# A hybrid decoder block on one core: earlier weight loads in the second half of the sparse branch, and a power on GpSimd as seed of the norms

## The chip, the cores and the metric

The kernel runs on one NeuronCore of one Trainium2 chip. What counts is the device time of one execution in microseconds (us). The engines are named as in the profile: PE (TensorE matmul, PEld its weight loads), DVE (VectorE), ACT (ScalarE), POOL (GpSimd) and SP (SyncE, which issues most of the DMAs). Each engine works through its own row of instructions in order; semaphores hold an instruction until what it reads is there.

## The reference, cut to what matters

One decoder block over 1024 tokens and 16 meta tokens of 1024 features, in float32:

```
def rms_norm(x, g):
    y = x * rsqrt(mean(x * x, axis=-1) + EPS)
    return y * g

hn = rms_norm(h, attn_norm_g)
proj = hn @ w_in                      # window q k v, latents of the sparse branch, indexer, gates
q = rms_norm(bq, q_norm_g) @ w_uq
c_kv = rms_norm(bkv, kv_norm_g)
ik = layer_norm(ik, idx_k_ln_g, idx_k_ln_b)
o_a = sliding_window_sink_attention(...)
o_b = indexed_sparse_mla(...)         # top 256 keys of each query, found by the indexer's scores
mixed = gate_a * (o_a @ w_branch_a) + gate_b * (o_b @ w_branch_b)
h = h + mixed @ w_out
hn = rms_norm(h, ffn_norm_g)
h = h + (silu(hn @ w_ffn_gate) * (hn @ w_ffn_up)) @ w_ffn_down
y = rms_norm(h, final_norm_g)
```

Each norm needs a reciprocal square root per token: for the two halves of the input (tiles `rx0`, `rx1`, 128 partitions x 5 columns), for the index keys (`rk`, 128 x 9), for the latents of the sparse branch (`rlat`, 128 x 18), and for each of eight blocks of 128 tokens before the feed-forward part and again at the end (`rh`, 128 x 1).

## The kernel before, in words

All large products are done as three matmuls of a high and a low part: ACT casts a tile to its high part, POOL or DVE subtracts to get the low part (`w_hi`, `w_lo` for weights in `weights`, L168 to L190; `fhl`, `th`, `tl`, `oh`, `ol` for other operands), and PE adds the three products in PSUM (`mm3`, L202).

The program is written as a sequence of phases: the norm of the input (`norm_x`, L398: sums of squares at L415, the mean at L417, `rsqrt` at L418, scaling at L424, PE transposes at L429), the indexer, the gates, the top-k search (`select_topk`, where `count` at L838 is done on DVE in rounds for the longest rows, and ACT, L880, and POOL, L824 and L888, search the others; L825 takes low halves), the latents (`latents`, L595, with `rsqrt` for `rlat` at L589 and the scaling L593), window attention, the sparse attention with the products `branch_a` and the first half of `branch_b`, then `phase_mix` (L1157): the second half of `branch_b`, a Winograd product with `w_out`, the norm before the feed-forward part (`squares` L1252, `row_scale` L1258, the scaling `xs` on ACT L1279, transposes to `s` on PE L1288, the copies `hb` on DVE L1291), the feed-forward part, and the last norm (`final`, L1525: `row_scale`, then `y` on ACT, L1533, with POOL, L1534, or on DVE, L1536).

The order on each engine isn't the order of the text: the whole program is placed by a scheduler that simulates a timeline (L1569), and the tiles' ring buffers (`bufs`) set which instruction must wait for which. So an edit in one place can move instructions in others.

A reciprocal square root is done on DVE alone. `rsqrt` takes a seed by two integer operations on the bits (L219, L220) and three Newton steps of three instructions (L222 to L224). `row_scale` makes `v` (L1264), the same seed (L1266, L1267), and three steps of two instructions (L1269, L1270); what its constants leave in scale is taken back in the gains (-1/256).

In the second half of `branch_b` the eight column blocks of `w_branch_b` are taken in the order of `HALF1` = 4, 5, 6, 7, 0, 1, 2, 3. The blocks 4 to 7 are still in the ring `w` of `WB` = 4 places from the first half. The blocks 0 to 3 are loaded again, each in the loop at its own turn, into that ring. Each unit loads a gate tile `ga` and a tile `gt` of the other branch, multiplies, and adds (`ga` L1140, `gt` L1141 in the profile's lines).

Of the kernel before, what the change touches and what calls it, by code (L numbers as in the profile page):

```python
# [7 lines left out]
F32 = mybir.dt.float32  # L8
F32R = mybir.dt.float32r
BF = mybir.dt.bfloat16  # L10
I32 = mybir.dt.int32
# [3 lines left out]
ALU = mybir.AluOpType  # L15
# [4 lines left out]
P = 128  # L20
D = 1024
KC = D // P
T = 1024
NB = T // P
# [26 lines left out]
WB = 4  # L51
# [52 lines left out]
class Program:  # L104
# [105 lines left out]
                    mm = self.matmul(ps, a, b, start=start and i + k == 0, stop=stop and i == n - 1 and k == 2, **kw)  # L210
        return mm.ins

    def rsqrt(self, pool, v, n, tag, e=0):

        nc = self.nc
        y = pool.tile([P, n], F32, name=f"{tag}_y", tag=f"{tag}_y", bufs=1)
        a = pool.tile([P, n], F32, name=f"{tag}_a", tag=f"{tag}_a", bufs=1)
        yi = y.bitcast(I32)
        nc.vector.tensor_scalar(yi, v.bitcast(I32), 1, None, op0=ALU.logical_shift_right)  # L219
        nc.vector.tensor_scalar(yi, yi, -1.0, float(0x5F3759DF + (e << 23)), op0=ALU.mult, op1=ALU.add)  # L220
        for _ in range(3):
            nc.vector.tensor_mul(a, y, y)  # L222
            nc.vector.scalar_tensor_tensor(a, a, -0.5 / 4 ** e, v, op0=ALU.mult, op1=ALU.mult)
            nc.vector.scalar_tensor_tensor(y, a, 1.5, y, op0=ALU.add, op1=ALU.mult)  # L224
        return y

    def run(self):
# [6 lines left out]
    def setup(self, tmp):  # L234
        nc, I, const = self.nc, self.I, self.const
        self.ident = const.tile([P, P], F32, name="ident")
        make_identity(nc, self.ident)
        rows = sum(n for _, n in VEC_ROWS)
        self.vec = const.tile([P, rows], F32, name="vec")
# [6 lines left out]
        at = 0  # L246
# [11 lines left out]
        nc.tensor.transpose(pt[:, :rows], raw, self.ident[:rows, :rows])  # L258
        nc.vector.tensor_copy(self.vec, pt[:, :rows])
        g = self.col["ffn_norm_g"]  # L260
        nc.vector.tensor_scalar(self.vec[:, g:g + 8], self.vec[:, g:g + 8], -1.0 / 256, None, op0=ALU.mult)
        g = self.col["b_gates"]
        nc.vector.tensor_scalar(self.vec[:, g:g + 16], self.vec[:, g:g + 16], 0.5, None, op0=ALU.mult)
        g = self.col["q_norm_g"]
# [859 lines left out]
    def branch_b(self, half, gp, marks=None):  # L1124

        nc, I, pool = self.nc, self.I, self.wg
        o = self.load_o(pool, self.ob_dram[half], 2, lo_pool=False, ring=gp if half else self.xhp, bufs=4 if half else 8)
        banks = ((self.gp, "gps"), (self.tp, "tp"), (self.sp, "s"), (self.tp, "tp"), (self.sp, "s"))
        for at, m in enumerate(HALF1 if half else range(KC)):
            if half == 0 or m < KC - WB:  # L1130
                self.wb[m] = self.weights(pool, I["w_branch_b"][0][:, P * m:P * m + P].rearrange("(k p) n -> p k n", p=P), raw_pool=pool, unit=512, bufs=WB)
            w = self.wb[m]
            y, g = [gp.tile([P, 512], F32, name=nm, tag=nm, bufs=GB if half else 2) for nm in ("gt", "ga")]
            nc.sync.dma_start(g, self.gate_dram[half][8 + m])
            self.mixed_in = nc.sync.dma_start(y, self.ya_dram[half][m]).ins
            bank, tag = banks[m % len(banks) if half else 0]
            ps = bank.tile([P, 512], F32, name=tag, tag=tag)
            self.mm3(ps, [(*w[k], *o[k]) for k in range(4)], marks)
            if half:
                nc.vector.tensor_mul(g, g, ps)  # L1140
                nc.vector.tensor_add(self.X[f"2{m // 4 + 1}"][:, m % 4], y, g)  # L1141
                self.load_out_weights(at)
            else:
                nm = ("oh", "ol")[m % 2]
                self.mixed.append(self.xhp.tile([P, 512], F32, name=nm, tag=nm, bufs=8))
                nc.vector.tensor_mul(g, g, ps)
                nc.gpsimd.tensor_add(self.mixed[m], y, g)

    def load_out_weights(self, at):

# [107 lines left out]
    def row_scale(self, b):  # L1258


        nc = self.nc
        t = self.hp.tile([P, 3], F32, name="rh", tag="rh", bufs=4)
        v, y, z = [t[:, k:k + 1] for k in range(3)]
        nc.vector.tensor_scalar(v, self.ss[:, b, :1], self.ss[:, b, 1:], D * EPS, op0=ALU.add, op1=ALU.add)  # L1264
        yi = y.bitcast(I32)
        nc.vector.tensor_scalar(yi, v.bitcast(I32), 1, None, op0=ALU.logical_shift_right)  # L1266
        nc.vector.tensor_scalar(yi, yi, -1.0, float(0x5F3759DF), op0=ALU.mult, op1=ALU.add)  # L1267
        for s in (1, 2, 16):
            nc.vector.scalar_tensor_tensor(z, y, y, v, op0=ALU.mult, op1=ALU.mult)  # L1269
            self.scaled_dve = nc.vector.scalar_tensor_tensor(y, z, -3.0 * s * s, y, op0=ALU.add, op1=ALU.mult).ins  # L1270
        return y


# [169 lines left out]
    def ffn_down(self):  # L1443
# [3 lines left out]
        nc, I, kc = self.nc, self.I, NF // 2  # L1447
# [9 lines left out]
        sums, gain = {}, None  # L1457
        for name in ("m1", "m5", "m6", "m3", "m7", "m2", "m4"):
# [47 lines left out]
            if name == "m7":  # L1506
                gain = self.fwp.tile([P, D], F32, name="gain", tag="fs", bufs=2)
                nc.sync.dma_start(gain, I["final_norm_g"].unsqueeze(0).to_broadcast([P, D]))
                nc.gpsimd.tensor_scalar(gain, gain, -1.0 / 256, 1.0, op0=ALU.mult, op1=ALU.mult)
            for k, i in [(k, i) for i in range(4) for k in range(kc)] if last else [(k, i) for k in range(kc) for i in range(4)]:  # L1510
                c = slice(P * i, P * i + P)
                xh, xl, yh, yl = ops[k]
# [60 lines left out]
```

## Time and profile before

| | us |
|---|---|
| runs, median of 3 | 1484.69 |
| runs, lowest and highest | 1483.06, 1485.52 |
| profiled execution | 1482.89 |
| its span in the trace | 1480.7 |
| PE busy | 1380.9 (93% of the span) |
| DVE busy | 1002.8 (68%) |
| ACT busy | 817.0 (55%) |
| POOL busy | 609.9 (41%) |

The span runs from the first to the last instruction that the trace has; the profiled execution's own time is 2.2 us longer. All times below count from the start of the span. A busy PE is the sign of a stretch that PE bounds; where PE is idle, the row of its next instruction names in brackets how long it was idle and what ended the wait.

### The profile page before, as it was taken

How to read it: one execution, taken by the hardware profiler on the slowest of the kernel's cores; microseconds unless marked ns; L12 is line 12 of the kernel's file. 1: busy time of each engine (PE TensorE's matmuls, PEld its weight loads, DVE VectorE, ACT ScalarE, POOL GpSimd, SP SyncE). 2: the span in 40 equal slices, each digit the busy share in tenths (PEclk: the TensorE clock that was granted, in tenths of full speed). 3: DMA queues.
4: the chain of work that ended last, by engine and by line, in shares of the span. 5: the costliest groups of instructions: out<-in, count | busy, mean ns of one | idle time of the engine just before them, and what ended most of it. 6: DMA issues, size and time to landing. Idle time of an engine off the chain costs nothing.

```text
span 1480.7 us, 21298 instructions
## 1 busy us (share of the span) xinstructions
PE 1380.9 (93%) x6847; PEld 1149.3 (78%) x6847; DVE 1002.8 (68%) x2136; ACT 817.0 (55%) x1743; POOL 609.9 (41%) x873
## 2 busy tenths in 40 slices
PE   4999997698998899999899699999999999999997
PEld 3988985586776788888677578888888888888886
DVE  6258979556786796785797984445544547696585
ACT  5347977883896686785246633333333334444473
POOL 4135574446675556664200025554554554000004
PEclk9999999799999899999999899999999999999999
DMA  6421221256336555327912033332322338823332
GB/s 204 144 65 46 57 85 64 69 185 198 100 108 170 147 165 162 118 94 251 307 50 97 18 114 114 115 114 97 109 87 100 107 107 309 309 100 107 120 101 114
DMA packets 148038, 189.79 MB, mean 128 GB/s; under 512 B 11331, under 2 KB 95126, under 8 KB 147670
## 3 DMA queue, kind: packets, MB, share of 16 engines
q1 hardware_dynamic: 147568, 188.28, 39.3%
q8 instruction: 54, 0.88, 0.2%
q14 instruction: 58, 0.48, 0.1%
q0 software_dynamic: 160, 0.01, 0.0%
q10 hardware_dynamic: 198, 0.14, 0.0%
HBM read 133.49 MB, written 58.03 MB: 129 GB/s over the span
## 4 chain that ended last, share of the span: by engine, by line
PE 69%; DVE 14%; DMA 5%; issue 4%; ACT 3%; POOL 3%; SPq 1%; POOLq 0%; DVEq 0%; ACTq 0%
PE ps L193 28%; PE s L193 25%; PE gps L193 9%; DVE mask L838 3%; PE pv L1073 2%; DMA kraw<-bk_dram 1%; PE s L1031 1%; PE tp L1062 1%; PE tp L198 1%; POOL y L1534 1%; DVE ptl L133 1%; DVE pb L1035 1%; PE pv L193 1%; DMA ga<-gate_dram 1%; DVE hb L1291 1%
## 5 line engine op out<-in xcount | busy, mean ns | idle before, releaser
L1384 POOL TENSOR_TENSOR fhl<-fr,fhl 128x512 fp32r<-128x512 f32 x60 | 96.8, 1633 | 224.0 <-ACT fhl L1383 224.0
L1384 POOL TENSOR_TENSOR fhl<-fs,fhl 128x512 fp32r<-128x512 f32 x80 | 106.4, 1353 | 106.6 <-ACT fhl L1383 106.6
L193 PE MATMUL s<-ht,fhl 128*128 128x512 f32 x384 | 121.7, 393 | 0.7 <-ACT fhl L1383 0.4
L188 POOL TENSOR_TENSOR w_lo<-w_raw,w_hi 128x512 fp32r<-128x512 f32 x60 | 80.5, 1343 | 83.5 <-ACT w_hi L187 74.2
L193 PE MATMUL ps<-ht,fhl 128*128 128x512 f32 x320 | 101.1, 392 | 0.0
L193 PE MATMUL gps<-oh,w_hi 128*128 128x512 f32 x232 | 93.8, 404 | 4.5 <-ACT gt L938 4.3
L193 PE MATMUL gps<-ol,w_hi 128*128 128x512 f32 x232 | 92.0, 397 | 0.0
L193 PE MATMUL gps<-oh,w_lo 128*128 128x512 f32 x232 | 91.6, 395 | 0.0
L193 PE MATMUL s<-yhl,fhl 128*128 128x512 f32 x396 | 90.6, 389 | 0.0
L193 PE MATMUL ps<-yhl,fhl 128*128 128x512 f32 x396 | 90.3, 389 | 0.0
L1454 ACT CAST yhl<-wd 128x512 fp32r<-128x512 f32 x66 | 41.1, 622 | 88.1 <-PE ps L193 48.5
L193 PE MATMUL s<-h,fhl 128*128 128x512 f32 x272 | 87.6, 393 | 1.1 <-DVE hb L1291 1.1
L193 PE MATMUL ps<-h,fhl 128*128 128x512 f32 x256 | 82.9, 395 | 5.1 <-ACT h L1341 5.1
L133 DVE TENSOR_TENSOR ptl<-tp,pth 128x512 fp32r<-128x512 f32 (+2 forms) x112 | 70.6, 645 | 24.2 <-ACT pth L127 23.8
L193 PEld LDWEIGHTS s<-yhl,fhl 128*128 128x128 f32 x396 | 74.3, 188 | 15.5
L193 PEld LDWEIGHTS ps<-yhl,fhl 128*128 128x128 f32 x396 | 74.3, 188 | 15.5
L193 PEld LDWEIGHTS s<-ht,fhl 128*128 128x128 f32 x384 | 72.0, 188 | 18.4 <-ACT fhl L1383 1.3
L880 ACT ACTIVATE mask<-high,smallg 128x1040 bf16<-128x1040 int16 (+3 forms) x66 | 70.7, 1071 | 24.0 <-DVE high L825 13.3
L1383 ACT CAST fhl<-fr 128x512 fp32r<-128x512 f32 x66 | 39.8, 619 | 76.3 <-issue 36.1
L1455 DVE TENSOR_TENSOR yhl<-wd,yhl 128x512 fp32r<-128x512 f32 x66 | 45.5, 689 | 49.0 <-ACT yhl L1454 49.0
L193 PE MATMUL s<-lt,fhl 128*128 128x512 f32 x192 | 75.1, 392 | 0.0
L1383 ACT CAST fhl<-fs 128x512 fp32r<-128x512 f32 x88 | 54.6, 625 | 33.1 <-PE s L193 17.4
(496 smaller groups left out, 4203.0 us busy)
## 6 DMA issues: line engine op xcount, KB each, us to landing
fr<-in_w_ffn_gate SPq DMA_DIRECT2D x22, 512.0 KB, 4.0
fr<-in_w_ffn_up SPq DMA_DIRECT2D x22, 512.0 KB, 4.6
wd<-in_w_ffn_down SPq DMA_DIRECT2D x44, 256.0 KB, 5.0
da<-acts SPq DMA_DIRECT2D x44, 256.0 KB, 3.5
w_raw<-in_w_in SPq DMA_DIRECT2D x40, 256.0 KB, 3.1
act<-a SPq DMA_DIRECT2D x33, 256.0 KB, 2.1
da<-act SPq DMA_DIRECT2D x33, 256.0 KB, 3.9
acts<-s SPq DMA_DIRECT2D x33, 256.0 KB, 2.0
```

What stands on the lines that cost most here:

```text
L133: nc.vector.tensor_sub(lo, ps, hi.bitcast(F32))
L188: (nc.vector if lo_dve else nc.gpsimd).tensor_sub(t[1], t[2], t[0].bitcast(F32))
L193: mm = self.nc.tensor.matmul(*args, **kw)
L198: mm = self.nc.tensor.transpose(*args)
L838: nc.vector.tensor_scalar(self.mask[j], src[j], at[:, i:i + 1], None, op0=op, op1=ALU.add, accum_out=out[:, i:i + 1])
L880: nc.scalar.activation(self.mask[j], src[j], AF.Sign, bias=at[:, i:i + 1], scale=scale, accum_out=out[:, i:i + 1])
L1031: nc.tensor.matmul(ps[:, :n], q[k][:, h, qc:qc + P], kb[:, h, at:at + n], start=k == 0, stop=k == 1)
L1073: mm = nc.tensor.matmul(acc[:, e, :], v, t[k][:, 256 * i:256 * i + 256], start=r + i + k == 0, stop=False)
L1383: nc.scalar.copy(hi, a[name])
L1384: (nc.gpsimd if q else nc.vector).tensor_sub(lo, a[name], hi.bitcast(F32))
L1454: nc.scalar.copy(hi, src)
L1455: nc.vector.tensor_sub(lo, src, hi.bitcast(F32))
```

## The change

`rsqrt` takes its seed from one GpSimd instruction, a power with exponent -0.5 out of a constant tile `power`, and does one Newton step. `row_scale` does the same with one step of two instructions, and the gains carry -16. That is 20 power instructions in all. In the second half of `branch_b` the blocks 0 and 1 get places of their own (`wb_hi`, `wb_lo`, in the pool of that phase, with the low part on DVE) and are loaded ahead of the loop; the blocks 2 and 3 are loaded into the ring behind the matmuls of the first two units.

```diff
-    def rsqrt(self, pool, v, n, tag, e=0):
+    def rsqrt(self, pool, v, n, tag):
...
-        yi = y.bitcast(I32)
-        nc.vector.tensor_scalar(yi, v.bitcast(I32), 1, None, op0=ALU.logical_shift_right)
-        nc.vector.tensor_scalar(yi, yi, -1.0, float(0x5F3759DF + (e << 23)), op0=ALU.mult, op1=ALU.add)
-        for _ in range(3):
-            nc.vector.tensor_mul(a, y, y)
-            nc.vector.scalar_tensor_tensor(a, a, -0.5 / 4 ** e, v, op0=ALU.mult, op1=ALU.mult)
-            nc.vector.scalar_tensor_tensor(y, a, 1.5, y, op0=ALU.add, op1=ALU.mult)
+        nc.gpsimd.tensor_tensor(y, v, self.power[:, :n], op=ALU.pow)
+        nc.vector.tensor_mul(a, y, y)
+        nc.vector.scalar_tensor_tensor(a, a, -0.5, v, op0=ALU.mult, op1=ALU.mult)
+        nc.vector.scalar_tensor_tensor(y, a, 1.5, y, op0=ALU.add, op1=ALU.mult)
         return y
...
+        self.power = const.tile([P, 2 * NB + 2], F32, name="power")
+        nc.gpsimd.memset(self.power, -0.5)
...
-        nc.vector.tensor_scalar(self.vec[:, g:g + 8], self.vec[:, g:g + 8], -1.0 / 256, None, op0=ALU.mult)
+        nc.vector.tensor_scalar(self.vec[:, g:g + 8], self.vec[:, g:g + 8], -16.0, None, op0=ALU.mult)
...
+        if half:
+
+            for m in range(2):
+                self.wb[m] = self.branch_weights(gp, m, "wb", 2)
         for at, m in enumerate(HALF1 if half else range(KC)):
-            if half == 0 or m < KC - WB:
-                self.wb[m] = self.weights(pool, I["w_branch_b"][0][:, P * m:P * m + P].rearrange("(k p) n -> p k n", p=P), raw_pool=pool, unit=512, bufs=WB)
+            if half == 0:
+                self.wb[m] = self.branch_weights(pool, m)
...
             if half:
+                if at < 2:
+                    self.wb[2 + at] = self.branch_weights(pool, 2 + at)
                 nc.vector.tensor_mul(g, g, ps)
...
+    def branch_weights(self, pool, m, tag="w", bufs=WB):
+        src = self.I["w_branch_b"][0][:, P * m:P * m + P].rearrange("(k p) n -> p k n", p=P)
+        names = tag if tag == "w" else ("wb_hi", "wb_lo", "w_raw")
+        return self.weights(pool, src, tag=names, raw_pool=self.wg, unit=512, bufs=bufs, lo_dve=tag != "w")
...
         nc.vector.tensor_scalar(v, self.ss[:, b, :1], self.ss[:, b, 1:], D * EPS, op0=ALU.add, op1=ALU.add)
-        yi = y.bitcast(I32)
-        nc.vector.tensor_scalar(yi, v.bitcast(I32), 1, None, op0=ALU.logical_shift_right)
-        nc.vector.tensor_scalar(yi, yi, -1.0, float(0x5F3759DF), op0=ALU.mult, op1=ALU.add)
-        for s in (1, 2, 16):
-            nc.vector.scalar_tensor_tensor(z, y, y, v, op0=ALU.mult, op1=ALU.mult)
-            self.scaled_dve = nc.vector.scalar_tensor_tensor(y, z, -3.0 * s * s, y, op0=ALU.add, op1=ALU.mult).ins
+        nc.gpsimd.tensor_tensor(y, v, self.power[:, :1], op=ALU.pow)
+        nc.vector.scalar_tensor_tensor(z, y, y, v, op0=ALU.mult, op1=ALU.mult)
+        self.scaled_dve = nc.vector.scalar_tensor_tensor(y, z, -3.0, y, op0=ALU.add, op1=ALU.mult).ins
         return y
...
-                nc.gpsimd.tensor_scalar(gain, gain, -1.0 / 256, 1.0, op0=ALU.mult, op1=ALU.mult)
+                nc.gpsimd.tensor_scalar(gain, gain, -16.0, 1.0, op0=ALU.mult, op1=ALU.mult)
```

The scheduler moves more than the diff says. Three places matter below. In the changed kernel a line's number is one lower from the setup up to `branch_b`, and three to ten higher behind it.

On DVE, where the norm of the latents meets the search: `small`, `smallg` and `smalld` are the search's bounds, `high` and `sc` its scores, the 128x784 and 128x528 pieces belong to the rows that ACT and POOL search. Before, ahead of the first round of counts over `smalld`:

```order
261 L846 TENSOR_SCALAR smalld<-smalld 128x3
262 L825 SCALAR_TENSOR_TENSOR high<-high,smallg_1219,mask_149 128x784
263 L825 SCALAR_TENSOR_TENSOR sc_203<-sc_203,smallg_1219,mask_147 128x528
264 L848 TENSOR_SCALAR smalld<-smalld 128x3
265 L825 SCALAR_TENSOR_TENSOR high<-high,small,mask_150 128x912
266 L825 SCALAR_TENSOR_TENSOR high<-high,small,mask_148 128x656
267 L838 TENSOR_SCALAR mask_150,smalld<-high,smalld 128x912
```

and now:

```order
230 L845 TENSOR_SCALAR smalld<-smalld 128x3
231 L847 TENSOR_SCALAR smalld<-smalld 128x3
232 L824 SCALAR_TENSOR_TENSOR high<-high,small,mask_150 128x912
233 L824 SCALAR_TENSOR_TENSOR high<-high,small,mask_148 128x656
234 L837 TENSOR_SCALAR mask_150,smalld<-high,smalld 128x912
235 L824 SCALAR_TENSOR_TENSOR high<-high,small,mask_145 128x272
236 L837 TENSOR_SCALAR mask_148,smalld<-high,smalld 128x656
237 L824 SCALAR_TENSOR_TENSOR high<-high,smallg_1200,mask_149 128x784
238 L837 TENSOR_SCALAR mask_145,smalld<-high,smalld 128x272
239 L824 SCALAR_TENSOR_TENSOR sc_203<-sc_203,smallg_1200,mask_147 128x528
```

The 784 and 528 pieces have moved from ahead of the first round into it. At the search's end the scaled latents (`ck`, `qn`, L135) have moved too: from behind the three L804 and one L811 that follow the search to right behind its last round of counts.

On SP, the DMA issues of the second half of `branch_b`: `ga` and `gt` are its gate and merge tiles, `w_raw` the blocks of `w_branch_b` before they are split. Before:

```order
299 L1135 DMA gt<-ya_dram_99 128x512
300 L1134 DMA ga<-gate_dram_124 128x512
301 L1135 DMA gt<-ya_dram_100 128x512
302 L1134 DMA ga<-gate_dram_140 128x512
303 L1135 DMA gt<-ya_dram_108 128x512
...
307 L185 DMA w_raw<-in_w_branch_b 128x4x128 x2
308 L1134 DMA ga<-gate_dram_134 128x512
```

and now:

```order
297 L185 DMA w_raw<-in_w_branch_b 128x4x128
298 L1138 DMA gt<-ya_dram_107 128x512
299 L185 DMA w_raw<-in_w_branch_b 128x4x128
...
305 L1138 DMA gt<-ya_dram_99 128x512
306 L185 DMA w_raw<-in_w_branch_b 128x4x128
307 L1137 DMA ga<-gate_dram_124 128x512
308 L1138 DMA gt<-ya_dram_100 128x512
309 L1137 DMA ga<-gate_dram_140 128x512
```

The last load of weights stood behind the tiles 124, 140 and 133, and stands now ahead of 124; the four loads are spread out, where the last four came in two pairs.

On DVE, between the Winograd product and the feed-forward part (`rh` is the norm's scale, `hb` the transposed copy of the scaled blocks, `l`, `fs` and `fhl` operands of the feed-forward part). Before, the second four blocks:

```order
1330 L1269 SCALAR_TENSOR_TENSOR rh<-rh 128x1
1331 L1270 SCALAR_TENSOR_TENSOR rh<-rh 128x1
1332 L1267 TENSOR_SCALAR rh<-rh 128x1
1333 L1269 SCALAR_TENSOR_TENSOR rh<-rh 128x1
1334 L1270 SCALAR_TENSOR_TENSOR rh<-rh 128x1
1335 L1269 SCALAR_TENSOR_TENSOR rh<-rh 128x1 x2
...
1348 L1270 SCALAR_TENSOR_TENSOR rh<-rh 128x1 x2
1349 L1291 TENSOR_TENSOR hb_8851<-s,vec 128x4x128
```

and now:

```order
1266 L1277 SCALAR_TENSOR_TENSOR rh<-rh 128x1
1267 L1276 SCALAR_TENSOR_TENSOR rh<-rh 128x1
1268 L1349 TENSOR_TENSOR l_9701<-hb_8823,h_9656 128x512
...
1275 L1277 SCALAR_TENSOR_TENSOR rh<-rh 128x1
1276 L1276 SCALAR_TENSOR_TENSOR rh<-rh 128x1
1277 L1381 TENSOR_TENSOR fs<-fs,fr 128x512
1278 L1277 SCALAR_TENSOR_TENSOR rh<-rh 128x1
1279 L1298 TENSOR_TENSOR hb_8825<-s,vec 128x4x128
```

The run of small instructions ahead of `hb` is gone; two per block are left, spread among the large ones. On PE the 16 transposes of the first two blocks have moved from behind the product's last matmuls to ahead of its last group.

## Rows read from the trace of the kernel before

**Rows 1.** Windows: length; PE, PEld, DVE, ACT, POOL busy us; PE clock; DMA share; GB/s.

```profile
197.00:245.00 48.00, 48.00 (x209) 39.05 (x209) 44.91 (x127) 30.20 (x69) 33.01 (x76) 1.00 0.27 88
245.00:270.00 25.00, 4.76 (x20) 2.99 (x18) 24.10 (x68) 19.80 (x45) 11.25 (x40) 0.65 0.15 52
270.00:300.00 30.00, 28.41 (x121) 22.79 (x122) 10.79 (x18) 26.23 (x59) 13.73 (x46) 0.89 0.20 65
...
700.00:730.00 30.00, 24.75 (x103) 18.35 (x101) 20.01 (x30) 7.96 (x13) 8.90 (x7) 1.00 0.85 281
...
806.00:858.00 52.00, 37.38 (x179) 29.80 (x177) 49.30 (x113) 33.89 (x59) 0.00 (x0) 0.87 0.12 46
858.00:1441.00 583.00, 582.60 (x2544) 477.00 (x2543) 346.76 (x466) 230.98 (x419) 204.54 (x141) 1.00 0.39 133
```

**Rows 2.** Timeline of DVE, 8 to 40 us: start, duration, instruction, idle before.

```profile
12.77 0.17 DVE L417 TENSOR_SCALAR ss<-ss 128x5 f32<-128x5 f32 x1
...
16.92 2.73 DVE L424 TENSOR_SCALAR x<-x,rx_y 128x1024 f32<-128x1024 f32 x4
...
20.89 1.05 DVE L417 TENSOR_SCALAR ss<-ss 128x5 f32<-128x5 f32 x1
...
32.72 2.08 DVE L424 TENSOR_SCALAR x<-x,rx_y 128x1024 f32<-128x1024 f32 x3 [0.26 <-DVE rx_y L224]
```

**Rows 3.** Timeline of PE, 8 to 42 us.

```profile
17.73 0.48 PE L429 MATMUL tp<-ident,x 128*128 128x128 f32 x1 [7.88 <-DVE x L424]
25.55 0.66 PE L429 MATMUL tp<-ident,x 128*128 128x128 f32 x4 [2.01 <-DVE xt L135]
```

**Rows 4.** Groups of POOL: busy us, mean ns of one, idle before.

```profile
L890 POOL TENSOR_TENSOR smallg<-smallg 128x2 f32<-128x2 f32 x64 | 13.6, 213 | 5.0
...
L1534 POOL TENSOR_TENSOR y<-y,gain 128x1024 f32<-128x1024 f32 x5 | 11.9, 2397 | 61.2 <-ACT y L1533 61.2
```

**Rows 5.** Timeline of POOL, 0 to 42 us.

```profile
3.12 0.30 POOL masks.py:199 TENSOR_SCALAR_AFFINE_SELECT ident<-ident 128x128 f32<-128x128 f32 x1
```

**Rows 6.** Timeline of DVE, 185 to 275 us.

```profile
194.37 1.32 DVE L219 TENSOR_SCALAR rlat_y<-ssq 128x18 int32<-128x18 int32 x1
...
197.93 5.73 DVE L593 TENSOR_SCALAR lraw<-lraw,rlat_y 16x128 f32<-16x128 f32 x17
...
206.07 1.02 DVE L825 SCALAR_TENSOR_TENSOR high<-high,smallg,mask 128x784 uint16<-128x784 int16 x1
207.01 0.75 DVE L825 SCALAR_TENSOR_TENSOR sc<-sc,smallg,mask 128x528 uint16<-128x528 int16 x1
...
266.94 0.16 DVE L861 SCALAR_TENSOR_TENSOR small<-smalld,small 128x3 int32<-128x3 int32 x1
...
269.74 0.23 DVE L135 SCALAR_TENSOR_TENSOR ck<-tp,vec,ck 128x16 fp32r<-128x16 f32 x1
```

**Rows 7.** Waits, 245 to 300 us: total us, times, longest.

```profile
PE s L193 <- ACT qn L129: 13.4, 1, 13.4
...
PE tp L198 <- DVE ck L135: 6.9, 1, 6.9
```

**Rows 8.** Timeline of PE, 708 to 732 us.

```profile
717.40 0.50 PE L193 MATMUL s<-oh,w_hi 128*128 128x512 f32 x1 [2.09 <-ACT w_hi L187]
...
728.14 0.97 PE L193 MATMUL ps<-th,fhl 128*128 128x512 f32 x3 [1.55 <-DVE ga L1140]
```

**Rows 9.** Timeline of DVE, 785 to 845 us.

```profile
806.81 2.48 DVE L1291 TENSOR_TENSOR hb<-s,vec 128x512 f32<-128x512 f32 x4 [2.47 <-PE s L1288]
...
822.72 0.34 DVE L1269 SCALAR_TENSOR_TENSOR rh<-rh 128x1 f32<-128x1 f32 x2
...
826.57 0.69 DVE L1291 TENSOR_TENSOR hb<-s,vec 128x512 f32<-128x512 f32 x1 [1.86 <-PE s L1288]
```

**Rows 10.** Timeline of DVE, 1455 to 1482 us.

```profile
1473.37 0.21 DVE L1264 TENSOR_SCALAR rh<-ss 128x1 f32<-128x1 f32 x1 [0.85 <-ACT sq L1256]
...
1475.39 0.75 DVE L1536 SCALAR_TENSOR_TENSOR y<-h,rh,gain 128x512 f32<-128x512 f32 x1
```

## The prediction

> **What bounds the kernel now.** I read the windows first: they show in which stretches PE is full, and there only less PE work helps. From 858 to 1441 us PE is busy for 582.60 of 583.00 us, and from 197 to 245 for 48.00 of 48.00 [rows 1]. The change takes no matmul away, so such a stretch only passes on what was gained ahead of it. The gaps are where something can be won: the start (PE idle for 7.88 us ahead of its first transposes, 2.01 later) [rows 3], 245 to 270 (PE busy 4.76 of 25.00, granted clock 0.65), 700 to 730 (24.75 of 30.00, DMA share 0.85) and 806 to 858 (37.38 of 52.00, with DVE busy 49.30) [rows 1]. The waits and timelines then name what ends each gap. Of 245 to 270 that is one wait of 13.4 us for `qn` and one of 6.9 for `ck`, both by way of DVE [rows 7]; the reader sees `ck` written only at 269.74 [rows 6].
>
> **The price that no row shows** is D, one power on GpSimd, the hops to POOL and back included. The nearest rows are a multiply of 128x2, 0.213 us, and of 128x1024, 2.397 us [rows 4]: a fixed 0.21 and some (2397 - 213)/1022 = 2.1 ns for a column. With k times the work of a multiply for each column, D is about 0.2 + 0.0021 k n us for n columns. At k = 1 that is 0.2 for every use, at k = 100 1.3 for `rx` (5 columns), 4.0 for `rlat` (18) and 0.4 for `rh` (1). I take D = 0.5 all through, nearest to the small row; the ends are 0.2 and the k = 100 values. Nothing below zero is possible, since POOL must start an instruction.
>
> **Start.** The mean is there at 12.77 + 0.17 = 12.94, the scaling of `x` starts at 16.92 [rows 2]: 3.98 us for eleven DVE instructions, with a sum of squares between them. After: D and three instructions. At 3.98 for twelve pieces none takes more than about 0.3 on average, so 1.1 to 1.4, a gain of 2.6 to 2.9 at D = 0.5, and PE's 7.88 shrinks by as much. On POOL only one low part of the indexer's weights stands ahead, done by then. In the second half the mean starts at 20.89 and scaling at 32.72 [rows 2]: nearly 12 us, since the small instructions share DVE with the copies of the first half. Three instead of eleven let go several us earlier, but PE has the first half's work to do then and idles for 2.01 only. I take 3 for the start; 0 to 5 are the ends. The third norm, of the index keys, lies beside PE's full stretch and counts as nothing; if that cover went, it would cost D less eight small instructions, a gain at the D taken.
>
> **Latents and search.** From 194.37 to 197.93 the seed and the steps of `rlat` hold DVE, 3.56 us, the first instruction 1.32 long, so the other ten 0.22 each [rows 6]. After: D and 0.7, a gain of 2.4, or 1.3 if an instruction goes on being slowed as that first one is; I take 1.1, since POOL has other small work ahead of the power. Against it: the two low halves of 1.02 and 0.75 us [rows 6] stood where DVE waited for POOL, and stand now inside the first counting round; 1.8 us on the search's chain, as what is queued behind them is every later round. For it: `ck` and `qn` no longer wait behind the four or so large instructions after the search, between 266.94 and 269.74 [rows 6], so 2.8 us. Net 2 for PE in this stretch. With the start's 3 that would be 5 us at 270. From 270 to 300 PE has 28.41 of 30.00 us of work [rows 1], so it passes on; the mask work behind the search ends only by what the search itself gained (3 + 1.1 - 1.8). I take 4 for all up to window attention, bounds 0 and 8. ACT's half of the search starts its next rows late with those halves: what is late next if its rows become the last.
>
> **Sparse attention.** The scheduler reorders it without a reason in the diff. PE is nearly full there. Zero, plus or minus 3.
>
> **Second half of the branch.** PE waits 2.09 us for `w_hi`, late because its DMA landed late, and later 1.55 for a bank that `ga` on DVE frees [rows 8]. The last weight load now goes out ahead of the tiles 124, 140 and 133 on SP. The bytes are the same, though, and DMA is at 0.85 [rows 1], so the tiles come later by what the weights come earlier: `ga` is late next. Two low parts move from POOL to DVE, 0.69 each as another 128x512 there [rows 9]; DVE is idle for 10 of these 30 us [rows 1], which covers them. If that cover went they would cost 1.4. I take 2; bounds 0 and 4.5, the gap's 5.25 less a rest.
>
> **Norm before the feed-forward part.** DVE is the bound of 806 to 858 (49.30 of 52.00) [rows 1], idle for 2.47 ahead of the first `hb` and 1.86 ahead of the fifth [rows 9]. Six of nine instructions go for each of four blocks, 24 in all; two take 0.34 [rows 9], so up to 24 x 0.17 = 4.1, less where they overlap. The 1.86, a wait for `xs` behind the last `rh`, goes if the powers finish beside the large instructions, which at D = 0.5 they do: POOL has nothing in this stretch (0.00) [rows 1]. The first transposes and copies move ahead of the product's end, into the 2.47. That makes up to 8.4. I take 4, half, since PE's own 37 us must still fit the rest; bounds 0.5 and 7.
>
> **End.** From the end of `v` (1473.37 + 0.21) to `y` at 1475.39 [rows 10] eight instructions take 1.81 us, 0.23 each, all on the path. After: D and two of them. Gain 0.9; bounds -0.5 (D = 1.9) and 1.2. In the blocks before, powers queue on POOL behind four long multiplies, off the path.
>
> **Sum:** 4 + 0 + 2 + 4 + 0.9 = 10.9 us off 1482.89 makes 1472.0 for a profiled execution. That one stands 1.8 below the median of its runs, 1484.69; so I forecast **1474** for the median.
>
> **A rule against the change.** No row of POOL shows a first use that costs extra: the first AFFINE_SELECT took 0.30 [rows 5]. The Trainium skill, page GPSIMD Engine Reference, section 2.1 Instruction dispatch, says that the first call to a freshly loaded kernel pays some 6 us to load its code, with no instruction in the profile for it. By that rule, as an estimate from that page alone, the sum would be 4.9 instead of 10.9; the row of the first AFFINE_SELECT doesn't show such a cost, though it need not be a freshly loaded kernel.
>
> **Rivals.** (1) *The reordering gives it back:* the start's gain is met by the low halves in the counting round, the branch stays with its DMAs, the norm saves only the bound's 0.5 to 1.5, and sparse attention loses 3. The sum: 3 - 1.8 + 0 + 1.5 + 0.9 - 3 = 0.6, so 1484. For it: DMA at 0.85, and that PE is full ahead of the search. Against: DVE's load falls by over 100 instructions in places where it bounds. (2) *The power is slow* (slower): it is computed column by column at k = 300 or so. Then `rx` 3.4, `rlat` 11.5, `rh` 0.8 at the end and four in a row in the norm, 3.3: 3.4 + 11.5 + 3.3 + 0.8 = 19.0 less the 2.0 that D had in the sum, so 6 slower than before, 1491. It decides from k of about 190, where these terms eat the 10.9. For it: a power is no single operation of any row. Against: POOL's other small rows are all near 0.2. (3) *The first power is late* at the start, on the path from 12.94: by something between the 3.98 that it replaces [rows 2] and a second 7.88 of PE's idle time [rows 3], 6 in the middle. The sum is then 5 and the time 1480. The first AFFINE_SELECT speaks against it. (4) *The change doesn't do what it says:* the early loads wait in SP's row for their raw buffers, so the branch gains nothing; 1476, inside the forecast's range.
>
> **How the numbers follow.** The forecast with (4) 0.57, rival (1) 0.21, (2) 0.15, (3) 0.07. The forecast's own range, by the bounds of its terms not all at one end, is 1465 to 1481. The whole range reaches over (1) and (3) and leaves out most of (2): 1465 to 1489. No change means within 0.2%, 3 us, about what a measurement of this kernel can tell. Faster than 1481.7: nine tenths of the forecast, a quarter of (1), seven tenths of (3), 0.62. Slower than 1487.7: a fifth of (1), most of (2), 0.17. The rest 0.21.
>
> **What would show it.** In the changed profile: PE's first transpose near 15 instead of 17.73, `ck` at some 264 to 266, no PE wait for `w_hi` near 715, `hb` without 1.86 of idle, `y` of the last block 0.9 nearer to its `v`, and a row for the power: below 0.5 us for 128x1, or I am wrong in all of them. Wrong would also be a longer gap between 245 and 270, or one at 715 with `ga` as its end.

## The result, and the profile after

The changed kernel takes 1474.51 us (median of 6 runs, 1471.94 to 1475.89), the kernel before in the same comparison 1484.86. The ratio is 0.9927, with a 95% interval of 0.9916 to 0.9938: 9 to 12 us faster. The forecast was 1474. The trace is of an execution of 1474.35 us with a span of 1472.6.

The power's price stands in the rows of the tile `power` (line, engine, operation, count: ns lowest/median/highest, first and last start):

```profile
L1275 POOL TENSOR_TENSOR rh<-rh,power x16: 543/556/1964, 786.5 to 1466.2; 128x1 f32<-128x1 f32 x16
L218 POOL TENSOR_TENSOR rx_y<-ss,power x2: 1182/1196/1210, 12.7 to 22.5; 128x5 f32<-128x5 f32 x2
...
L218 POOL TENSOR_TENSOR rk_y<-var,power x1: 1795/1795/1795, 81.3 to 81.3; 128x9 f32<-128x9 f32 x1
L218 POOL TENSOR_TENSOR rlat_y<-ssq,power x1: 3248/3248/3248, 192.5 to 192.5; 128x18 f32<-128x18 f32 x1
```

These are 0.56 us for one column, 1.20 for five, 1.80 for nine and 3.25 for eighteen: about 0.40 and 0.158 for each column, some 75 times the 2.1 ns that a multiply takes for a column [rows 4].

The start, on DVE and then PE. The seed and step are over at 15.19, where `x` was scaled from 16.92 on [rows 2]; 0.35 of this lead is the mean itself, which is there at 12.59 and not 12.94. PE waits 5.33 instead of 7.88 [rows 3]:

```profile
12.42 0.17 DVE L416 TENSOR_SCALAR ss<-ss 128x5 f32<-128x5 f32 x1 [1.17 <-ACT junk L412]
13.91 0.84 DVE L219 TENSOR_TENSOR rx_a<-rx_y 128x5 f32<-128x5 f32 x1 [1.32 <-POOL rx_y L218]
...
15.19 2.73 DVE L423 TENSOR_SCALAR x<-x,rx_y 128x1024 f32<-128x1024 f32 x4
```
```profile
16.00 0.47 PE L428 MATMUL tp<-ident,x 128*128 128x128 f32 x1 [5.33 <-DVE x L423]
```

The latents, on DVE (answers to [rows 6]). `ssq`, the sums of squares of the latents, comes 3.1 us earlier (190.19, before 193.28), yet the scaling of `lraw` starts 0.7 later than before, since DVE waits 4.61 for the power and two small instructions are slowed to 1.34 and 1.22. `ck`, however, is written at 264.73 and not at 269.74:

```profile
190.19 0.96 DVE L586 TENSOR_SCALAR ssq<-ssq 128x9 f32<-128x9 f32 x1 [8.12 <-ACT junk L579]
195.76 0.18 DVE L219 TENSOR_TENSOR rlat_a<-rlat_y 128x18 f32<-128x18 f32 x1 [4.61 <-POOL rlat_y L218]
195.97 1.34 DVE L220 SCALAR_TENSOR_TENSOR rlat_a<-rlat_a,ssq 128x18 f32<-128x18 f32 x1
197.35 1.22 DVE L221 SCALAR_TENSOR_TENSOR rlat_y<-rlat_a,rlat_y 128x18 f32<-128x18 f32 x1
198.66 5.11 DVE L592 TENSOR_SCALAR lraw<-lraw,rlat_y 16x128 f32<-16x128 f32 x17
...
264.73 0.23 DVE L135 SCALAR_TENSOR_TENSOR ck<-tp,vec,ck 128x16 fp32r<-128x16 f32 x1
...
266.51 0.16 DVE L860 SCALAR_TENSOR_TENSOR small<-smalld,small 128x3 int32<-128x3 int32 x1
```

POOL in the same time: the power stands behind a low part, and the next two low parts run beside DVE's slowed steps:

```profile
191.24 1.28 POOL L188 TENSOR_TENSOR wa_lo<-wa_raw,wa_hi 128x512 fp32r<-128x512 f32 x1
192.48 3.25 POOL L218 TENSOR_TENSOR rlat_y<-ssq,power 128x18 f32<-128x18 f32 x1
...
195.99 2.54 POOL L188 TENSOR_TENSOR wa_lo<-wa_raw,wa_hi 128x512 fp32r<-128x512 f32 x2
```

The second half of the branch, PE and then DVE (answers to [rows 8]). No wait for `w_hi` is left; PE's waits of 2.7 us in sum for it are gone. But its wait for `ga` grew from 1.55 to 3.49 and its wait for `tl` from 1.09 to 3.70, so that PE's waits sum to 7.2 us where some 5.4 were. Ahead of the first, DVE stood for the output weights:

```profile
715.04 0.80 PE L193 MATMUL gps<-oh,wb_hi 128*128 128x512 f32 x1 [3.49 <-DVE ga L1145]
725.52 0.79 PE L193 MATMUL ps<-tl,fhl 128*128 128x512 f32 x1 [3.70 <-DVE tl L133]
```
```profile
710.57 2.50 DVE L1222 TENSOR_TENSOR w<-w,w 128x512 f32<-128x512 f32 x4 [4.34 <-DMA w<-in_w_out]
```

The two waits hang together by TensorE's clock. After the 3.49 us of idle time the granted clock is 0.50, the lower of its two levels (1.2 GHz); the last gate product takes 12 matmuls some 0.43 us apart, where those before the wait are 0.23 apart, and DVE waits for it, ahead of the sums that `tl` needs. Before, after 2.09 us of idle time, the same window has the clock at 1.00, the upper level (2.4 GHz). The windows (columns as in [rows 1]) of the kernel before and then of the changed kernel; of the changed kernel also two matmuls from ahead of the wait, two from behind it, and DVE:

```profile
715.00:720.00 5.00, 2.75 (x11) 1.60 (x10) 3.59 (x7) 1.24 (x2) 2.52 (x2) 1.00 0.96 336
```
```profile
715.00:720.00 5.00, 4.96 (x12) 3.89 (x13) 2.76 (x4) 0.62 (x1) 0.00 (x0) 0.50 0.85 251
```
```profile
710.72 0.39 PE L193 MATMUL gps<-ol,w_hi 128*128 128x512 f32 x1
710.94 0.39 PE L193 MATMUL gps<-oh,w_lo 128*128 128x512 f32 x1
...
716.06 0.63 PE L193 MATMUL gps<-oh,wb_lo 128*128 128x512 f32 x1
716.49 0.63 PE L193 MATMUL gps<-oh,wb_hi 128*128 128x512 f32 x1
```
```profile
720.57 0.69 DVE L1145 TENSOR_TENSOR ga<-ga,gps 128x512 f32<-128x512 f32 x1 [2.02 <-PE gps L193]
```

The norm before the feed-forward part on DVE (answers to [rows 9]): the fifth block's `hb` and the first wait no longer, but the copies of the third and fourth do, for 3.16.

```profile
805.29 0.69 DVE L1298 TENSOR_TENSOR hb<-s,vec 128x512 f32<-128x512 f32 x1 [3.16 <-PE s L1295]
...
819.06 1.28 DVE L1298 TENSOR_TENSOR hb<-s,vec 128x512 f32<-128x512 f32 x2
```

The end, all engines (answers to [rows 10]): from the end of `v`, 1466.14, to `y` at 1467.25 are 1.11 us, where 1.81 were.

```profile
1465.93 0.21 DVE L1274 TENSOR_SCALAR rh<-ss 128x1 f32<-128x1 f32 x1 [0.85 <-ACT sq L1266]
1466.22 0.55 POOL L1275 TENSOR_TENSOR rh<-rh,power 128x1 f32<-128x1 f32 x1 [4.50 <-DVE rh L1274]
1466.80 0.22 DVE L1276 SCALAR_TENSOR_TENSOR rh<-rh 128x1 f32<-128x1 f32 x1 [0.66 <-POOL rh L1275]
1467.06 0.16 DVE L1277 SCALAR_TENSOR_TENSOR rh<-rh 128x1 f32<-128x1 f32 x1
1467.25 0.75 DVE L1543 SCALAR_TENSOR_TENSOR y<-h,rh,gain 128x512 f32<-128x512 f32 x1
```

To put times to the parts, each trace is divided at four landmarks that every kernel has, taken from the views of their tiles on DVE: the first reciprocal `sua` of window attention, the last reciprocal `rs` of sparse attention, the first low part `tl` of the Winograd product, and the last low part `xl` of the feed-forward part. The traces of all twelve experiments stand here; what they are is told below. Each is of one execution.

| us | to `sua` | to `rs` | to `tl` | to `xl` |
|---|---|---|---|---|
| before | 368.0 | 299.5 | 62.0 | 711.9 |
| changed | 364.1 | 295.9 | 64.8 | 709.1 |
| changed, second trace | 365.5 | 299.8 | 64.8 | 708.8 |
| branch alone (e1) | 369.5 | 301.0 | 63.2 | 712.0 |
| all norms, no branch (e2) | 363.6 | 300.0 | 59.8 | 708.4 |
| `rsqrt` alone (e3) | 364.8 | 300.9 | 61.2 | 711.8 |
| `row_scale` alone (e4) | 369.2 | 303.8 | 62.8 | 705.9 |
| changed, `rlat` on DVE (f1) | 365.4 | 300.2 | 63.5 | 708.7 |
| changed, `rlat` in halves (f2) | 373.2 | 297.1 | 65.9 | 708.7 |
| changed, `ck` held back (g1) | 363.8 | 300.9 | 63.7 | 708.9 |
| `ck` first, `rlat` on DVE (g2) | 357.8 | 302.0 | 61.9 | 707.4 |
| `ck` first, all powers (g3) | 351.5 | 298.2 | 60.8 | 708.4 |
| changed, `w` behind (i1) | 365.0 | 299.8 | 65.6 | 709.2 |
| g2, `w` behind (i2) | 357.5 | 300.4 | 63.1 | 709.2 |

### The profile page after: what moved, and what is told of

Read it like the earlier page. It is cut to its first block, busy times and chain, and to the rows that moved or that the text cites. A ratio compares the mean times of both kernels' runs of the same rounds, so it can differ in the third digit from the quotient of the medians.

```text
span 1472.6 us, 21190 instructions
## 1 busy us (share of the span) xinstructions
PE 1383.2 (94%) x6847; PEld 1153.4 (78%) x6847; DVE 985.3 (67%) x2010; ACT 816.1 (55%) x1743; POOL 634.9 (43%) x892
## 5 line engine op out<-in xcount | busy, mean ns | idle before, releaser
L1275 POOL TENSOR_TENSOR rh<-rh,power 128x1 f32<-128x1 f32 x16 | 12.5, 797 | 167.3 <-DVE rh L1274 164.3
L879 ACT ACTIVATE mask<-high,smallg 128x784 bf16<-128x784 uint16 (+3 forms) x66 | 70.6, 1070 | 18.2 <-DVE smalld L854 8.4
```

The lines of the kernel that those rows point to most:

```text
L879: nc.scalar.activation(self.mask[j], src[j], AF.Sign, bias=at[:, i:i + 1], scale=scale, accum_out=out[:, i:i + 1])
L1275: nc.gpsimd.tensor_tensor(y, v, self.power[:, :1], op=ALU.pow)
```

## The experiments

**The parts of the change.** Four kernels have one or two of its three parts:

```diff
 e1:  branch_b as in the changed kernel; rsqrt and row_scale as before
 e2:  rsqrt and row_scale as in the changed kernel; branch_b as before
 e3:  rsqrt alone as in the changed kernel
 e4:  row_scale and the gains alone as in the changed kernel
```

*The branch alone.* 

> The kernel before with the edit of the branch's weights alone, norms as they were. Order of instructions is that of before up to the second half of the branch. Three theories. (a) The prediction's term: PE no longer waits 2.09 us for w_hi, the branch gains 2 us: 1482.9 against 1484.9. (b) DMA at 0.85 bounds this stretch: the gate tiles come later by what the weights come earlier, no change within 1 us. (c) The edit costs: in the changed kernel PE's two waits there, 3.5 for ga and 3.7 for tl, sum to more than the five of before (5.3), so 1485 to 1487. Under (b) the trace shows no wait for w_hi, and one for ga or tl of the same sum, 4.7 to 5.9 us of idle PE from 700 to 731.

Measured: 1488.65 against 1485.75, ratio 1.0015 (1.0003 to 1.0027): slower by 0.4 to 4 us, so (a) falls. The interval fits (c) and reaches into (b)'s 1 us. PE's waits from 695 to 736 us (total, times, longest) are for other things and no shorter, some 6 where some 5.4 were:

```profile
PE ps L193 <- DVE tl L133: 2.6, 1, 2.6
PE gps L193 <- DVE ga L1146: 2.3, 1, 2.3
PE ps L193 <- DVE ga L1146: 1.1, 1, 1.1
```

*The norms without the branch.* 

> The changed kernel with the branch's weights loaded as before; power seeds in all norms. Under (a) of the run before 1476.5 (2 slower than the changed kernel, 1474.5), under (b) 1474.5 within 1 us, under (c) 1472.5 to 1474. The gain up to 690 us, some 8 us in the trace, should be there in all cases, since the branch's edit can't reach back; the offset behind the branch tells the three apart: 4 us as in the changed kernel under (b), 2 under (a), 6 under (c).

Measured: 1473.88, ratio 0.9920 (0.9907 to 0.9933), no different from the changed kernel's 0.9927 by the intervals. But the stretch from `rs` to `tl` is 59.8 against 64.8, the sign of (c). What the edit costs in one pair of traces differs (5.0 here, 1.2 between e1 and before). Over all traces that stretch is 63.2 to 65.9 in the seven with the edit (mean 64.5) and 59.8 to 63.1 in the seven without (61.7): on average the edit costs 2.8 us where it acts.

*rsqrt alone.* 

> The kernel before with the power seed in rsqrt alone (input, index keys, latents); blocks' norms and the branch as before. If the parts add up, the changed kernel's 0.9927 is the product of 1.0015 (branch alone), 0.9978 (blocks alone) and this one, so 0.9934, 1475 to 1477 against 1485; its trace has the first window attention (sua) some 4 us earlier than before. Rival: the parts don't add, since each one reorders the program: a ratio of 0.997 or more would mean that start and latents alone give little, below 0.991 that they give all.

Measured: 1478.96, ratio 0.9953 (0.9941 to 0.9965): it misses both, between the sum's 0.9934 and the rival's 0.997; `sua` is at 364.8, 3.2 us earlier than before. The product of the three parts, 0.9953 x 0.9978 x 1.0015 = 0.9946, lies within their errors of the changed kernel's.

*row_scale alone.* 

> The kernel before with the power seed in row_scale alone (eight blocks before the feed-forward part, eight at the end). By the stretches of five traces, from the first low part of the Winograd product to the end of the feed-forward part these sixteen give 3.2 us and the end another 0.6: 1481 against 1484.9. Rivals: the predicted 4.9 (1480), or that with the start as before nothing of it is left (1484.9).

Measured: 1483.20 against 1485.78, ratio 0.9978 (0.9965 to 0.9991): 1.3 to 5.2 us, which holds the expected 3.8 and the predicted 4.9. From `tl` to `xl` all kernels with this part take 705.9 to 709.2, those without 711.8 to 712.0.

**The changed kernel again**, the same program:

```diff
 (none)
```

> The changed kernel once more, as a second trace of it and as the mark for the runs of this chip: 1474 to 1475 by its six runs. Two theories on its faster sparse stretch (4 us less from the first window attention to the last output of the sparse attention in its trace than before, while the same order without the branch's edit had none of it): if it comes from the order of instructions, this trace shows it again within 1 us; if it is the scatter of one execution, it differs by 2 us or more.

Measured: 1477.06 (1473.93 to 1479.66), 2 above what was expected, with a ratio of 0.9936 (0.9919 to 0.9953) that agrees with the first. The sparse stretch takes 299.8 and not 295.9, with the same instructions: the second theory. The 4 us in the first trace were scatter of one execution, and differences below that between two single traces of this stretch tell nothing.

**The seed of the latents.** In f1 `rlat` goes back to DVE, in f2 its power is split:

```diff
 f1:
+        if tag == "rlat":
+            (shift, multiply and three steps on DVE as before)
+        else:
             nc.gpsimd.tensor_tensor(y, v, self.power[:, :n], op=ALU.pow)
 f2:
-        nc.gpsimd.tensor_tensor(y, v, self.power[:, :n], op=ALU.pow)
+        step = NB + 1 if tag == "rlat" else n
+        for at in range(0, n, step):
+            nc.gpsimd.tensor_tensor(y[:, at:at + step], v[:, at:at + step], self.power[:, :step], op=ALU.pow)
```

*On DVE.* 

> The changed kernel with the old DVE seed and three steps for rlat alone (128x18); the other norms keep the power. Theory: the power of 18 columns costs 3.25 us behind two low parts on POOL, and DVE idles 4.6 for it, so the scaling of the latents starts some 3 to 4 us earlier than in the changed kernel (195 instead of 198.7); the end of the search and of ck follow by 3, and the whole is 1471 to 1473. Rival: the wait is hidden, because the stretch from 245 to 300 is ended by the search of ACT and POOL and not by DVE: 1474.5 within 1 us though the scaling starts earlier.

Measured: 1477.41, ratio 0.9939 (0.9927 to 0.9951): not faster than the changed kernel. DVE's timeline shows why: the scaling does start 3.8 us earlier, the search ends 2.8 earlier, but `ck` was placed behind the counts that follow the search, and is written 1.8 later than at 264.73:

```profile
194.82 5.27 DVE L598 TENSOR_SCALAR lraw<-lraw,rlat_y 16x128 f32<-16x128 f32 x15
...
263.76 0.16 DVE L866 SCALAR_TENSOR_TENSOR small<-smalld,small 128x3 int32<-128x3 int32 x1
...
266.56 0.23 DVE L135 SCALAR_TENSOR_TENSOR ck<-tp,vec,ck 128x16 fp32r<-128x16 f32 x1
```

So the power's delay is hidden here, as the rival said, though by the order and not by the other engines' searches. The traces of the other kernels point the same way: `sua` goes with `ck` and not with the search's end. With the old seeds `ck` is written at 269.4 to 269.9 and the search ends at 266.6 to 267.1; in the six kernels' traces with the powers `ck` comes at 264.7 to 265.6 while the search ends at 265.5 to 266.9, nearly as before, and `sua` comes 4.4 earlier.

*In halves.* 

> The changed kernel with rlat's power in two instructions of nine columns, the first ready some 11 us before the second. By the line through the powers seen (1.20 us at 5, 1.80 at 9, 3.25 at 18 columns) each takes 1.8; the second alone is on the path, so the scaling starts 1.4 earlier or more, if the first is placed ahead of the low parts: 1473 to 1474 where the wait for rlat reaches the end, 1474.5 within 1 us where it is hidden (the rival of the run before).

Measured: 1483.74, ratio 0.9986 (0.9976 to 0.9995), 7 to 9 us slower than the changed kernel by the ratios, which neither theory allowed. The order did it: the second `ssq` is formed at 200.8 instead of 190.2, and `sua` is at 373.2. The trace shows what held it up. The first half of the power stands in POOL's row ahead of the search's small instructions and waits there for the first `ssq`; the search on ACT waits for what stands behind it, and the squares that the second `ssq` needs (`junk`) are queued behind the search on ACT. POOL and then ACT:

```profile
180.85 1.82 POOL L220 TENSOR_TENSOR rlat_y<-ssq,power 128x9 f32<-128x9 f32 x1 [12.67 <-DVE ssq L588]
```
```profile
184.08 0.95 ACT L881 ACTIVATE mask<-high,smallg 128x784 bf16<-128x784 int16 x1 [11.02 <-POOL smallg L891]
```

An edit of two instructions can cost more by the order that the scheduler makes of it than it could ever win by itself.

**The place of the latents.** g1 holds the first `ck` and `qn` back behind the search's last instruction; g2 (with `rlat` on DVE, no branch edit) and g3 (with all powers, no branch edit) write the latents ahead of the rest of the search:

```diff
 g1:
+                with self.tc.issue_after(self.search_end) if c0 == 2 or (bs[0] == 0 and c == 0) else nullcontext():
                     self.split(pt[:, :n * len(bs)], *[t[:, at:at + n * len(bs)] for t in dst], scale=scales[c])
...
-        nc.vector.scalar_tensor_tensor(tb, d, 0, tb, op0=ALU.bitwise_xor, op1=ALU.bitwise_xor)
+        self.search_end = nc.vector.scalar_tensor_tensor(tb, d, 0, tb, op0=ALU.bitwise_xor, op1=ALU.bitwise_xor).ins
 g2, g3:
+            self.latents(lp)
             next(search, None)
             self.window_inputs(lp)
-            self.latents(lp)
```

*Held back.* 

> The changed kernel with one constraint: the first scaled latents on DVE (ck of the meta tokens and the first qn) are issued behind the search's end, where they stood in the kernel before and in the run with rlat seeded on DVE. Theory: the place of ck, not the seed of rlat, carries the gain of the latents; the scaling starts at 198.7 as in the changed kernel, but ck is written some 2 us later (267 instead of 264.7) and PE's two waits end that much later; the whole is 1476 to 1478. Rival: what ends the stretch from 245 to 300 is the search itself, which ends a little earlier here, and the order of ck is worth nothing: 1474.5 within 1 us.

Measured: 1479.07 beside the changed kernel's 1477.06 on the same chip, ratios 0.9957 (0.9940 to 0.9973) and 0.9936 (0.9919 to 0.9953), which overlap. The constraint was weaker than meant: `ck` went right behind the search's end, ahead of the counts, and came at 265.6, 0.9 late; `sua` was not late at all (363.8). That tells neither theory from the other.

*First, with `rlat` on DVE.* 

> The power in all norms but rlat's (DVE, as before), the branch as before, and the latents written into the program ahead of the second part of the search, so that ck and qn are issued among the first counting rounds. Theory: DVE's in-order row is what holds PE idle from 245 to 270; with ck first PE's 18 to 20 us of waits there go, the search's end moves later by the copies' 4.5 us, and if PE's work and not the search ends the phase, 10 us or more are won: 1460 to 1470. Rival: the search's end starts the mask work for the window and sparse attention, which then ends the phase, 4 to 5 us later: 1477 to 1482.

Measured: 1470.35, ratio 0.9895 (0.9879 to 0.9911): the theory, 0.4 us above the upper end of its range. *First, with the power:* 

> As the run with ck first (1470.4), but with the power for rlat too, as in the changed kernel. Theory: rlat's power of 3.25 us delays the scaling by 3.5 to 4 us (198.7 against 194.8); with ck no longer queued behind the search, this delay moves the search's end and reaches the end of the phase: 1473 to 1475. Rival: it is hidden as it was in the changed kernel, 1470 to 1471.

Measured: 1465.48 (1458.99 to 1469.52), ratio 0.9876 (0.9849 to 0.9904), below both theories on the power's price here. By the median it isn't slower than g2, but the two intervals overlap, so that it is faster isn't shown. Its trace is of the fastest of its six executions, 6.5 us below their median. The windows of 245 to 270 us (columns as in [rows 1]), of g2 and of g3, against 4.76 us of PE at a clock of 0.65 before:

```profile
245.00:270.00 25.00, 16.99 (x66) 12.56 (x65) 24.00 (x72) 23.24 (x54) 11.70 (x44) 0.93 0.16 61
```
```profile
245.00:270.00 25.00, 22.65 (x100) 17.95 (x100) 23.79 (x74) 25.00 (x58) 13.11 (x48) 1.00 0.33 115
```

The hole that bounded this phase is mostly filled in g2 and all but gone in g3, at full clock. It was DVE's row: the latents sat behind the search. Why the trace of g3 fills it better than that of g2 stays open. g3 beats both kernels of this study, by 1.2% the one before.

**The sums over the output weights.** If DVE's wait of 4.34 for `w`, with gate products behind it, is what the branch edit costs, moving the sums behind the last gate product gives it back:

```diff
-                nc.vector.tensor_mul(g, g, ps)
+                self.gated = nc.vector.tensor_mul(g, g, ps).ins
...
-                combine(b, "t1", "12", "12", "11", sub)
+                with self.tc.issue_after(self.gated) if done else nullcontext():
+                    combine(b, "t1", "12", "12", "11", sub)
```

*On the changed kernel.* 

> The changed kernel with one constraint on DVE: the four sums over the output weights (w, 2.5 us of work, which waited 4.3 us for their DMA with gate products of the branch behind them) are issued behind the branch's last gate product. Theory: with the early weight loads the in-order row of DVE is what holds PE, so PE's wait of 3.5 for ga goes and the stretch from the last reciprocal of the sparse attention (rs) to the first low part of the Winograd product (tl), 64.8 in both traces of the changed kernel, falls to 61 to 62, as without the edit; 2 to 3 us off the changed kernel. Rival: the tiles themselves are late since DMA is near 0.9 there; the wait moves to ga's DMA, 64 to 65 as before, and the time is that of the changed kernel.

Measured: 1476.26, ratio 0.9948 (0.9933 to 0.9963), the stretch 65.6: time and stretch are the rival's. DVE's timeline has the wait on the next thing:

```profile
717.07 0.69 DVE L1145 TENSOR_TENSOR ga<-ga,tp 128x512 f32<-128x512 f32 x1 [6.10 <-DMA ga<-gate_dram]
```

The constraint has a price of its own, though: PE's wait for `ga` fell from 3.5 to 2.8, and its wait for `tl`, which the sums now precede, rose from 3.7 to 6.5. So the run shows that this move wins nothing. It doesn't show that a busy DMA is what makes `ga` late, and the traces speak against that. In the changed kernel SP issues nothing for over 5 us, and the DMA engines stand empty from 699 to 702 (share 0.00), just ahead of the late tiles. SP, and the window:

```profile
696.17 0.38 SPq L1138 DMA_DIRECT2D gt<-ya_dram  x1
701.61 0.32 SPq L1137 DMA_DIRECT2D ga<-gate_dram  x1
```
```profile
699.00:702.00 3.00, 3.00 (x15) 2.49 (x14) 3.00 (x5) 1.76 (x3) 2.27 (x2) 1.00 0.00 0
```

The gate tiles are issued late, then, and not moved slowly: from issue to landing they take 6.2 us (median) and took 7.9 before. SP waits for places in their ring (`GB` = 3), which come free when DVE (for the first half of the branch, DVE and POOL) has used the tiles. All fourteen traces divide by the edit. In the seven with it DVE's first gate product of the second half (`ga<-ga,s`) starts 39.5 to 40.6 us after `rs`, the fifth gate load from the end goes out at 41.5 to 42.6, and the DMA is empty for 3.5 to 4 us between 30 and 48; in the seven without it these are 34.3 to 35.3, 37.1 to 38.3 and 0.5 to 1.5. The order on PE is a likely reason: with the weights of the early blocks there, PE runs nine matmuls with `wb_hi` and `wb_lo` and a product of the first half (693.03 to 698.87) before the last matmuls of that gate product. No run changes this order alone, so this reason is argued and not shown.

*On g2.* 

> The run with ck first (1470.4, no edit of the branch) with the same constraint on the sums over w. Without the edit DVE waits 2.8 us there with one gate product behind it, and PE's waits are for w_hi (2.2 in sum) and tl (2.2); so at most 1 to 2 us are won, 1468.5 to 1470.4; if the sums at the end are on the path to tl, 1471 to 1473.

Measured: 1472.44, ratio 0.9920 (0.9898 to 0.9942), the stretch 63.1 against 61.9. The intervals of g2 and i2 overlap; in the trace the sums at the end are on the path to `tl`, whose wait grew from 2.2 to 5.0 us.

## Why the prediction was right, and where not

**The sum, and the range:** 10.9 us off by the forecast, 9 to 12 measured. The faster case held. But that the number is so near is in part luck, since two errors met each other. By the runs all norms together (e2) give 11.9 us (10.0 to 13.8) where 4 + 4 + 0.9 = 8.9 were predicted, and the branch (e1) costs 2.2 where it was to give 2.

**Start and latents, 4 predicted.** Right as a whole: `sua` comes at a mean of 364.5 in the six traces with these powers and their usual order (the changed kernel twice, e2, e3, g1, i1), 368.9 in the three with the old seeds (before, e1, e4); 4.4 us. e3's runs, which have these powers alone, give 7.0 (5.2 to 8.8). Inside, the start gave 1.7 at the first transposes and 3.1 by `ssq`, for a predicted 3. The step that failed is *"I take D = 0.5 all through"*: D was 0.56 only for one column. For `rx` it was 1.20, near the k = 100 end, and for `rlat` 3.25. So the term of `rlat`, a predicted gain of 1.1, is a loss: 3.1 of lead turned into 0.7 of lag, 3.8, made of the power, of its place behind low parts, and of two slowed steps. What paid for it is the order: `ck` ahead of the counts, predicted at 2.8, with the whole of 5.0 at `ck`. f1, where the loss and that place go together, ends up the same, and `sua` follows `ck` in the traces; a run with the loss alone taken away is missing. The mask work was to end earlier by what the search gained, 2.3; the search ends only 0.4 earlier (266.51 against 266.94), and `sua` didn't wait for it.

**Sparse attention, 0 plus or minus 3.** Within its bounds: 299.8 and 295.9 against 299.5, with a scatter of 4 from one execution to the next.

**The branch, a gain of 2 predicted.** Wrong in sign: it costs 2.8 on average in its stretch, and e1 alone is 0.4 to 4 slower. The step that failed is *"I take 2; bounds 0 and 4.5"*. What it had named as late next, `ga`, is what came: PE's waits for `w_hi`, 2.7 in sum, went, and those for `ga` and `tl` grew by 1.9 and 2.6. The reason that it gave for `ga`, the same bytes at a DMA share of 0.85, isn't what the traces show: the gate tiles went out 3.3 to 3.7 us later after `rs` than before, with the DMA empty ahead of them, as their places came free later. That the clock falls in PE's longer wait, which makes `tl` late too, was not in the prediction. A bound below nothing was missing.

**The norm before the feed-forward part, 4 predicted.** Right in size: `tl` to `xl` falls from 711.9 (three traces) to a mean of 708.4 (eleven), 3.5 us. Of the two waits that were to go, the 1.86 is gone; in place of the 2.47 there is one of 3.16, ahead of the third block's copies. The 4 was half of three gains taken together, so that it fits owes something to the choice of the half.

**The end, 0.9 predicted:** 1.81 to 1.11, 0.7.

**Its own signs.** No wait for `w_hi`, `ck` at 264 to 266 and `hb` without the 1.86 came as written, and the gap from 245 to 270 is no longer than before (PE busy for 7.04 us of it, 4.76 before). The first transpose came at 16.00 and not near 15. Two signs of being wrong came true: the power takes 0.54 us or more for 128x1, where "below 0.5" was the mark, and there is a wait at 715 with `ga` as its end. So the total was right with the term of the branch wrong by its own sign.

**Rivals.** The power's k is about 75 and lies below the 190 where it decides. The first power is not late: 1.21 us at 12.67, the second 1.18. The Trainium skill, page GPSIMD Engine Reference, section 2.1 Instruction dispatch, has some 6 us for the first call to a freshly loaded kernel. This trace shows no such cost, so either the power isn't such a kernel or it was loaded ahead; no run here tells which. Rival (1) is right on the branch, which gave nothing, but not on the rest. Rival (4) has the branch's outcome, no gain, but not its way: the last weight load went out 31.3 us after `rs`, where it was 40.7 before.

**What stays open.** By the landmarks the parts sum to 4.4 + 3.5 + 0.7 - 2.8 = 5.8 us, where the ratios of the two comparisons of the changed kernel give 9.5 and 10.8. Another 0.4 lies outside the span (2.2 us of the execution before, 1.8 after). Taken to `rs` instead of `sua`, the same nine traces differ by 6.3 and not 4.4 (670.3 against 664.0), which is nearer to e3's 7.0; so some 2 us may come in the sparse attention. Its scatter in single traces is larger than that, so this isn't shown.

## What to carry to other kernels

Price an operation that no row shows for each size in which it is used, and not once: a fixed part and a part for each column, with both ends. Where a scheduler sets the order, look first at which engine's row the starved engine's input is queued in; here the place of a few copies was worth more than the price of any instruction, and writing the latents ahead of the search gave some 6.5 us more (g3's ratio of 0.9876 against 0.9920 of e2, which has the same norms and the same branch). When a load is moved ahead, ask what its reader will then do sooner, and whose places come free later for it: here two early weight loads made the gate tiles' loads go out over 3 us later, though a DMA share of 0.85 over the stretch made the DMA look like the limit. An instruction that is placed too early in an engine's row stops what stands behind it: half a power on POOL held the search on ACT for 11 us.

## What was not expected of the hardware

- A small DVE instruction of 128x18 takes 0.18 us alone. Where one started together with a POOL subtraction of 128x512, it ended with it: 1.34 and 1.22 beside two of them that take 2.54 (195.97 and 195.99), and 1.32 beside one of 1.30 in the kernel before (194.37 [rows 6] and 194.36), 1.31 beside one of 1.29 in f1 (191.28 and 191.26). A seed that is moved to POOL leaves fewer instructions to be slowed, but not cheaper ones.
- After PE's wait of 3.49 us for `ga` the granted clock was 0.50 for the next 12 matmuls. They took some 2.4 us more than at 1.00, as an estimate from the 0.43 and 0.23 us between their starts; the price of a wait doesn't end with it.
- The power on GpSimd grows by 0.158 us for each column of 128 partitions, so it is a cheap seed for 128x1 (0.56 us) and a dear one for 128x18 (3.25).
